# Sixteen expert buffers, a later branch, contiguous rows and unread products around the routing

## The chip, the core and the metric

The kernel runs on one NeuronCore of a Trainium2 chip, as one program. The metric is device time in microseconds of one execution; lower is better. Five engines matter: PE (TensorE), DVE (VectorE), ACT (ScalarE), POOL (GpSimd) and SP (SyncE, which here mostly issues DMA transfers). Each runs its own instructions in order, and they wait for each other through semaphores.

## What is computed

Two transformer blocks on 256 tokens of width 1024, all in fp32. The change lies in the last part of the second block, a mixture of 16 experts:

```python
def hier_moe(h, w_rg, b_rg, w_re, b_re, w1, w3, w2):
    t = h.reshape(-1, d)
    lg = (t @ w_rg + b_rg).astype(jnp.float32)
    g_sel = jnp.argmax(lg, axis=-1)
    w_grp = jnp.take_along_axis(jax.nn.softmax(lg, axis=-1), g_sel[:, None], axis=-1)
    le = (t @ w_re + b_re).astype(jnp.float32).reshape(-1, N_GROUPS, EXPERTS_PER_GROUP)
    le_g = jnp.take_along_axis(le, g_sel[:, None, None], axis=1)[:, 0]
    top_v, top_i = lax.top_k(le_g, TOP_K_IN_GROUP)
    w_top = jax.nn.softmax(top_v, axis=-1) * w_grp
    ...
    def expert_step(acc, xs):
        y = (jax.nn.silu(t @ w1e) * (t @ w3e)) @ w2e
        return acc + ge[:, None] * y, None
...
    x_lat = x_lat + g2 * hier_moe(h2_l, ...)
    return rmsnorm(x_lat, final_g)
```

Each token goes to two of the four experts of one group. One expert has three weight matrices of 2 MiB each (gate, up, down); the 16 experts together have 96 MiB, all of which are read.

## The kernel before

The program runs once through the first block (FFN, attention and recurrence, FFN), then through the second (modulation, attention, output products) and reaches the mixture at about 915 us. There it works in these stages.

**Routing.** The token rows are two tiles x[b] of 128 x 1024. `x_turn` transposes them on PE (trp), `x_high` (L1707) writes a rounded copy of x times its norm into xnh on ACT and `x_low` (L1711) the rest into xnl on DVE; both permute the columns, four interleaved sets per half of 512, so that later reads are contiguous. `logits(b)` (L1716) are eight products of 20 columns (lgp). `pick(b)` (L1726) finds, on DVE, group and ranks and writes m16, two for each token's chosen experts. Three rank products (L1766 to L1768) count the places within the experts, and `one_hot` (L1772) compares them with 0 to 63, so that each expert has 64 places. A token that finds no place is an overflow, counted into novi. The gate weights are worked out beside that by POOL, with one exponential on ACT and one reciprocal on DVE; they end in ghl, which the products gsl (L1810) read.

**Experts.** They go in eight pairs, two experts side by side on PE, each with 64 rows. `gather(p)` (L1788), for two pairs at once, makes the gathered rows, transposed, by one-hot products (gat: for each of eight k four products, weights are columns of xnh and xnl), and evacuates them to xe with scale and shift. Then, per pair: `gate(p)` (pg), `down(p-1)` (yacc), `up(p)` (pu), the gather of the next two pairs if it is due, the transposes of the one-hots (oht), the products that put the rows of p-1 back onto x (scat), and the transposes of the hidden rows (eT, copied by ACT to hT). `down(7)` stands alone at the end. PE's order in this loop is the order of the code.

**Loads.** Each pair has 12 loads of 1 MiB (128 x 2048 fp32), 96 in all, issued by SP from `load_rows` (L234) in the order gate(p), down(p-1), up(p). Buffers are taken in turn from three sets, 5 of tag rawa, 4 of the ring raw that the earlier weights use too, and 4 of rawb: 13. A load whose buffer isn't free makes SP wait, and all behind it.

**Overflow.** `overflow()` (L1895) reads novi into a register on every engine and branches: the body runs the overflowing tokens through all experts, with its own weight loads from SP. With these inputs the count is zero and the body is jumped over. It is called at p == 6, behind hidden_T(6); ahead of it the loads of gate(7), down(6) and up(7) are issued (L2009), and the four of down(7) are issued behind it. On SP the end of the branch also waits for loads in flight.

**End.** `scatter(7)` adds the last rows, then the final RMS norm (squares on ACT, powers on POOL, products on DVE) and four output transfers. The final gain is loaded at about 855 us by POOL into K4[2]. K4 are four fp32 tiles of 128 x 1024.

What sets the order: DVE and ACT stand in the order of the code in the routing (manual schedule `route`), PE in the pair loop; elsewhere a scheduler places instructions by its own estimate.

Of the kernel before, what the change touches and what calls it, by code (L numbers as in the profile page):

```python
# [9 lines left out]
F32 = mybir.dt.float32  # L10
# [23 lines left out]
def constants():  # L34
# [66 lines left out]
    moe={"4": 4, "xe": 2, "oh": 2, "h": 3, "1": 2, "m": 16}, raws=(5, 4, 4))  # L101
# [16 lines left out]
def _body(tc, nc, es, I, out, dbg, stop, R):  # L118
# [116 lines left out]
    def load_rows(src, k):  # L235

        n, i = R["raws"], nraw[0] % sum(R["raws"])
        if i < n[0]:
            raw = P["raw1"].tile([128, 2048], F32, name="rawa", tag="rawa", bufs=n[0])
        elif i < n[0] + n[1]:  # L240
            raw = raw_tile()
        else:
            raw = P["raw2"].tile([128, 2048], F32, name="rawb", tag="rawb", bufs=n[2])
# [189 lines left out]
    x = []  # L433
# [13 lines left out]
    K4 = [cp.tile([128, 1024], F32, name=f"K{i}") for i in range(4)]  # L447
# [1206 lines left out]
    g1b, g2b = K4[1], K4[3]  # L1654
# [22 lines left out]
    route = tc.manual_schedule(engines={mybir.EngineType.DVE, mybir.EngineType.Activation})  # L1677
# [26 lines left out]
    rows4 = lambda t: t.rearrange("p (h q j) -> p h j q", h=2, j=4)  # L1704
    tiles4 = lambda t: t.rearrange("p (h j q) -> p h j q", h=2, j=4)

    def x_high(b):  # L1707
        for h in range(2):
            ACT.activation(tiles4(xnh[b])[:, h], rows4(x[b])[:, h], AF.Copy, scale=rsx[:, b:b + 1])

    def x_low(b):  # L1711
        for h in range(2):
            DVE.scalar_tensor_tensor(tiles4(xnl[b])[:, h], rows4(x[b])[:, h], rsx[:, b:b + 1], tiles4(f32(xnh[b]))[:, h],
                                     op0=OP.mult, op1=OP.subtract)
# [9 lines left out]
    by4 = lambda t: t.rearrange("p b (g e) -> p b g e", g=4)  # L1724

# [19 lines left out]
    for b in range(2):  # L1745
        x_high(b)
        logits(b)
    x_low(0)
# [18 lines left out]
    mm(pr[:, 16:32], ltr[:, 128:256], m16[:, 0, :], start=True, stop=False)  # L1767
    mm(pr[:, 16:32], ltr[:, 0:128], m16[:, 1, :], start=False, stop=True)  # L1768

# [11 lines left out]
    fg = K4[2]  # L1781
    nc.gpsimd.dma_start(fg, bass.AP(tensor=I["final_g_2"].tensor, offset=I["final_g_2"].offset, ap=[[0, 128], [1, D]]))
# [5 lines left out]
    def gather(p):  # L1788

        t = alloc("xe", 2048, "xe", F32, "")  # L1790
        for u in range(2):
            xe[p + u] = lambda k, u=u: t[:, 256 * k + 128 * u:256 * k + 128 * u + 128]
        for k in range(8):
            if k % 2 == 0:
                ps = pa("gat")
            o, s_ = ps[:, 256 * (k % 2):256 * (k % 2) + 256], slice(128 * k, 128 * k + 128)
# [283 lines left out]
```

## Time and profile before

| | us |
|---|---|
| three runs | 1177.48, 1183.94, 1184.63 (median 1183.94) |
| profiled execution | 1180.25 |
| its span on the core | 1178.5 |
| PE busy in the span | 1108.8 (94%) |
| DVE, ACT, POOL busy | 621.2, 477.3, 60.7 |
| bytes moved by DMA | 262.98 MB, mean 223 GB/s |

A profile is one execution, taken by the hardware profiler. A timeline row has the start and the length in us, the engine, the line of the kernel, the operation, the tiles (written <- read), the shape and the count; in brackets how long the engine had stood idle before it and which instruction released it. PE is the product, PEld the load of its weights. A row of a table of stretches has the stretch, its length, the busy time of PE, PEld, DVE, ACT and POOL in it with the instructions in parentheses, PEclk, DMA and GB/s. PEclk is TensorE's granted clock as a share of full speed (1.00 is 2.4 GHz, 0.50 is 1.2 GHz), DMA the busy share of the 16 DMA engines, GB/s what they moved.

### The profile page before, as it was taken

The numbers are of one execution on the slowest core, as the hardware profiler recorded it, in microseconds if no ns is written. First come the engines' busy times: TensorE is split into PE (matmuls) and PEld (weight loads), VectorE is DVE, ScalarE is ACT, GpSimd is POOL, SyncE is SP. The second block draws the span as 40 slices with busy tenths as digits, with TensorE's granted clock in tenths as the row PEclk, the third lists the DMA queues.
The fourth block names the chain that finished last, engine by engine and source line by source line (L and its number), as shares of the span: only waits on it lengthen the run. The fifth ranks groups of instructions, "written<-read, shape, count | busy, mean of one in ns | idle before, by whom it ended". The sixth has DMA issues, their size and how long they took to land. (4 is left out here: it accounts for less than half of the span.)

```text
span 1178.5 us, 17991 instructions
## 1 busy us (share of the span) xinstructions
PE 1108.8 (94%) x7527; PEld 870.1 (74%) x7527; DVE 621.2 (53%) x928; ACT 477.3 (40%) x711; POOL 60.7 (5%) x106
## 2 busy tenths in 40 slices
PE   6999999998988999999999999999899799999976
PEld 6999997887756888999998688888898534343432
DVE  4545545556976556455445865666656603232314
ACT  5444444476643355444444445555544300100002
POOL 1000001000330001000000100000000200000000
PEclk9999999999988999999999999999999799999988
DMA  9855654453557548555556454214285399999984
GB/s 338 275 191 179 198 180 158 157 169 112 179 197 261 197 139 304 195 179 185 175 191 218 153 179 160 72 55 152 96 327 210 145 366 419 421 420 420 421 354 175
DMA packets 119538, 262.98 MB, mean 223 GB/s; under 512 B 6873, under 2 KB 83802, under 8 KB 105242
## 3 DMA queue, kind: packets, MB, share of 16 engines
q1 hardware_dynamic: 118506, 258.88, 60.7%
q0 software_dynamic: 656, 2.36, 0.6%
q8 instruction: 61, 1.00, 0.3%
q10 hardware_dynamic: 288, 0.52, 0.1%
q14 instruction: 27, 0.22, 0.1%
HBM read 260.70 MB, written 1.05 MB: 222 GB/s over the span
## 5 line engine op out<-in xcount | busy, mean ns | idle before, releaser
L263 DVE TENSOR_TENSOR lo<-raw,hi 128x1024 fp32r<-128x1024 f32 x243 | 297.2, 1224 | 285.9 <-ACT hi L262 285.5
L262 ACT ACTIVATE hi<-raw 128x1024 fp32r<-128x1024 f32 x246 | 260.6, 1060 | 318.2 <-PE pj L227 203.3
L227 PE MATMUL pj<-H,hi 128*128 128x256 f32 x752 | 212.4, 283 | 4.1 <-issue 4.1
L226 PE MATMUL pj<-H,hi 128*128 128x256 f32 x752 | 216.2, 288 | 0.0
L228 PE MATMUL pj<-H,lo 128*128 128x256 f32 x752 | 212.4, 282 | 0.4 <-POOL lo L263 0.4
L226 PEld LDWEIGHTS pj<-H,hi 128*128 128x128 f32 x752 | 142.8, 190 | 8.5 <-issue 4.5
L228 PEld LDWEIGHTS pj<-H,lo 128*128 128x128 f32 x752 | 143.0, 190 | 5.2 <-issue 4.5
L227 PEld LDWEIGHTS pj<-H,hi 128*128 128x128 f32 x752 | 142.7, 190 | 1.3 <-issue 0.5
L228 PE MATMUL pj<-hTh,lo 128*128 128x256 f32 x352 | 99.4, 283 | 0.1
L227 PE MATMUL pj<-hTl,hi 128*128 128x256 f32 x352 | 99.2, 283 | 0.0
L226 PE MATMUL pj<-hTh,hi 128*128 128x256 f32 x352 | 99.1, 283 | 0.0
L227 PEld LDWEIGHTS pj<-hTl,hi 128*128 128x128 f32 x352 | 67.3, 192 | 1.3 <-DVE hTl L509 0.8
L226 PEld LDWEIGHTS pj<-hTh,hi 128*128 128x128 f32 x352 | 67.2, 192 | 1.2 <-ACT hTh L508 0.8
L228 PEld LDWEIGHTS pj<-hTh,lo 128*128 128x128 f32 x352 | 67.4, 192 | 0.3 <-DVE lo L263 0.3
L1881 DVE TENSOR_TENSOR yf<-yacc,K 128x512 f32<-128x512 f32 x16 | 11.0, 691 | 104.7 <-PE yacc L1832 82.5
L404 PE MATMUL acc<-lo,hTh 128*128 128x512 f32 x160 | 63.1, 394 | 0.0
L403 PE MATMUL acc<-hi,hTh 128*128 128x512 f32 x160 | 62.7, 392 | 0.0
L407 PE MATMUL acc<-hi,hTl 128*128 128x512 f32 x160 | 49.9, 393 | 0.0
L1832 PE MATMUL pu<-rawa,xe 128*64 128x512 f32 x160 | 45.3, 605 | 0.0
L1864 ACT ACTIVATE hT<-eT 128x512 f32<-128x512 f32 x8 | 4.8, 597 | 91.6 <-PE eT L1863 91.6
L1832 PE MATMUL pg<-raw,xe 128*64 128x512 f32 x128 | 35.8, 595 | 0.0
L1832 PE MATMUL yacc<-rawb,hT 128*64 128x512 f32 x128 | 35.5, 592 | 0.0
(496 smaller groups left out, 1895.2 us busy)
## 6 DMA issues: line engine op xcount, KB each, us to landing
raw<-in_w_in_dram SPq DMA_DIRECT2D x43, 1024.0 KB, 5.1
raw<-in_ffn_up_dram SPq DMA_DIRECT2D x22, 1024.0 KB, 5.2
raw<-in_ffn_down_dram SPq DMA_DIRECT2D x22, 1024.0 KB, 4.9
raw<-in_ffn_gate_dram SPq DMA_DIRECT2D x21, 1024.0 KB, 5.2
rawa<-in_w_exp_up_dram SPq DMA_DIRECT2D x20, 1024.0 KB, 19.2
raw<-in_w_exp_gate_dram SPq DMA_DIRECT2D x16, 1024.0 KB, 14.1
rawb<-in_w_exp_down_dram SPq DMA_DIRECT2D x16, 1024.0 KB, 17.5
raw<-in_w_mod_dram SPq DMA_DIRECT2D x15, 1024.0 KB, 5.0
```

Of the source, the lines that this page charges most:

```text
L226: mm(o, l[0], r[0], start=first, stop=False)
L227: mm(o, l[0], r[1], start=False, stop=False)
L228: mm(o, l[1], r[0], start=False, stop=last)
L262: ACT.activation(hi, r, AF.Copy)
L263: low = lambda: (sub or DVE).tensor_tensor(lo, r, f32(hi), op=OP.subtract)
L403: mm(ps[b][n], hh, wh[:, s_], start=first and f == 0, stop=False)
L404: mm(ps[b][n], hh, wl[:, s_], start=False, stop=False)
L407: mm(ps[b][n], ll, wh[:, s_], start=False, stop=last and f == 1)
L1832: mm(o[halves[u]], l[:, 64 * u:64 * u + 64], r[u], start=first, stop=last, tile_position=(0, 64 * u))
L1864: ACT.activation(t, ps, AF.Copy)
L1881: tt(part(yf, n), yaccs[p][n], part(g2b, n), op=OP.mult)
```

## The change

It has five parts.

- **Buffers.** The expert loads take 16 buffers in turn: 5 rawa, one made of K4[0] and K4[1] (K01), 4 raw, 6 rawb. Room for them comes from smaller pools: tag "4" of the stage from 4 tiles to 2, xe from 2 to 1. g1b moves to a tile of tag "4", yf to K4[2], the tiles of the final norm to xe and K4. The load of the final gain, which sat in K4[2], now goes into K4[0] behind the pair loop.
- **Branch.** overflow() is called at p == 7, behind hidden_T(7) and behind the issue of the down(7) loads, and its body's loads are issued by ACT.
- **Rows.** x_high and x_low no longer permute; each is one instruction of 1024 contiguous elements. The gather reads its weights with a stride of four columns instead.
- **Unread products.** `keep_busy` multiplies ident with g2b into a PSUM tile that nothing reads, 256 or 512 columns wide, at five places between logits and rank products; the routing's written order now covers PE too.
- **Evacuation.** Odd k of the gather are evacuated by ACT, even k by DVE; one_hot(b, 4, 12) stands behind the gather. The first four steps of down(7) come in the order of the other pairs.

```diff
--- before.py
+++ after.py
@@ -98,7 +98,7 @@
     ffn={"4": 16, "2": 11, "1": 2, "m": 12},
     mid={"r4": 9, "r2": 6, "r1": 7, "rm": 16, "v4": 3, "s4": 6, "sm": 6, "gm": 4, "m2": 2, "mm": 2, "pm": 4, "cm": 4, "c1": 2},
     blk={"4": 9, "2": 5, "1": 7, "m": 25}, att={"4": 6, "2": 9},
-    moe={"4": 4, "xe": 2, "oh": 2, "h": 3, "1": 2, "m": 16}, raws=(5, 4, 4))
+    moe={"4": 2, "xe": 1, "oh": 2, "h": 3, "1": 2, "m": 16}, raws=(5, 1, 4, 6))
 
 
 class Stop(Exception):
@@ -238,9 +238,11 @@
         if i < n[0]:
             raw = P["raw1"].tile([128, 2048], F32, name="rawa", tag="rawa", bufs=n[0])
         elif i < n[0] + n[1]:
+            raw = K01
+        elif i < n[0] + n[1] + n[2]:
             raw = raw_tile()
         else:
-            raw = P["raw2"].tile([128, 2048], F32, name="rawb", tag="rawb", bufs=n[2])
+            raw = P["raw2"].tile([128, 2048], F32, name="rawb", tag="rawb", bufs=n[3])
         nraw[0] += 1
         nc.sync.dma_start(raw, src.rearrange("(p k) n -> p (k n)", k=k))
         return raw
@@ -444,7 +446,8 @@
                        channel_multiplier=-1)
 
     H = [cp.tile([128, 1024], F32R, name=f"H{i}") for i in range(4)]
-    K4 = [cp.tile([128, 1024], F32, name=f"K{i}") for i in range(4)]
+    K01 = cp.tile([128, 2048], F32, name="K01")
+    K4 = [K01[:, 0:1024], K01[:, 1024:2048]] + [cp.tile([128, 1024], F32, name=f"K{i}") for i in (2, 3)]
     nhalf = cp.tile([128, 32], F32, name="nhalf")
     POOL.memset(nhalf, -0.5)
     nones = cp.tile([128, 128], F32, name="nones")
@@ -1651,7 +1654,7 @@
     att.close()
     P["raw1"] = es.enter_context(tc.tile_pool(name="raw1", bufs=1, side="right", reuse_waits="tile"))
 
-    g1b, g2b = K4[1], K4[3]
+    g1b, g2b = t4("gb"), K4[3]
     part = lambda t, n: t[:, 512 * n:512 * n + 512]
     for n in range(2):
         ACT.activation(part(g1b, n), mod_bcast(mhl[0], n), AF.Copy)
@@ -1674,7 +1677,7 @@
     L, rsx = cp.tile([128, 2, 20], F32, name="L"), cp.tile([128, 2], F32, name="rsx")
     xnh, xnl, xT = H[0:2], H[2:4], [t4("xT") for _ in range(2)]
     pl = pa("lgp")
-    route = tc.manual_schedule(engines={mybir.EngineType.DVE, mybir.EngineType.Activation})
+    route = tc.manual_schedule(engines={mybir.EngineType.DVE, mybir.EngineType.Activation, mybir.EngineType.PE})
     route.__enter__()
 
     def x_add(b):
@@ -1701,17 +1704,12 @@
                 ACT.activation(part(xT[b], kh), ps, AF.Copy)
 
 
-    rows4 = lambda t: t.rearrange("p (h q j) -> p h j q", h=2, j=4)
-    tiles4 = lambda t: t.rearrange("p (h j q) -> p h j q", h=2, j=4)
 
     def x_high(b):
-        for h in range(2):
-            ACT.activation(tiles4(xnh[b])[:, h], rows4(x[b])[:, h], AF.Copy, scale=rsx[:, b:b + 1])
+        ACT.activation(xnh[b], x[b], AF.Copy, scale=rsx[:, b:b + 1])
 
     def x_low(b):
-        for h in range(2):
-            DVE.scalar_tensor_tensor(tiles4(xnl[b])[:, h], rows4(x[b])[:, h], rsx[:, b:b + 1], tiles4(f32(xnh[b]))[:, h],
-                                     op0=OP.mult, op1=OP.subtract)
+        DVE.scalar_tensor_tensor(xnl[b], x[b], rsx[:, b:b + 1], f32(xnh[b]), op0=OP.mult, op1=OP.subtract)
 
     def logits(b):
         for k in range(8):
@@ -1722,6 +1720,11 @@
     rk, sel = cp.tile([128, 2, 5, 4], F32, name="rk"), cp.tile([128, 2, 4], F32, name="sel")
     m16 = cp.tile([128, 2, 16], F32R, name="m16")
     by4 = lambda t: t.rearrange("p b (g e) -> p b g e", g=4)
+
+    def keep_busy(n, w=512):
+
+        for _ in range(n):
+            mm(pa("busy")[:, 0:w], ident, g2b[:, 0:w], start=True, stop=True)
 
     def pick(b):
         DVE.scalar_tensor_tensor(L[:, b], pl[:, 32 * b:32 * b + 20], rsx[:, b:b + 1], rbias, op0=OP.mult, op1=OP.add)
@@ -1745,6 +1748,8 @@
     for b in range(2):
         x_high(b)
         logits(b)
+        keep_busy(1, 256)
+    keep_busy(2)
     x_low(0)
     pick(0)
     x_low(1)
@@ -1765,7 +1770,9 @@
     pr = pa("rank")
     mm(pr[:, 0:16], ltr[:, 0:128], m16[:, 0, :], start=True, stop=True)
     mm(pr[:, 16:32], ltr[:, 128:256], m16[:, 0, :], start=True, stop=False)
+    keep_busy(2)
     mm(pr[:, 16:32], ltr[:, 0:128], m16[:, 1, :], start=False, stop=True)
+    keep_busy(1, 256)
 
     oh = [alloc("oh", 1024, "oh", F32R, "") for _ in range(2)]
 
@@ -1778,8 +1785,6 @@
         one_hot(b, 0, 4)
     pr16 = big("pr16")
     DVE.tensor_copy(pr16, pr[:, 0:32].rearrange("p (b n) -> p b n", b=2))
-    fg = K4[2]
-    nc.gpsimd.dma_start(fg, bass.AP(tensor=I["final_g_2"].tensor, offset=I["final_g_2"].offset, ap=[[0, 128], [1, D]]))
     gsl = sm("gsl", 8)
     novi = mp.tile([1, 1], I32, name="novi", tag="novi", bufs=1)
     xe, hps, yaccs, hTs, backs = {}, {}, {}, {}, {}
@@ -1790,16 +1795,21 @@
         t = alloc("xe", 2048, "xe", F32, "")
         for u in range(2):
             xe[p + u] = lambda k, u=u: t[:, 256 * k + 128 * u:256 * k + 128 * u + 128]
+        pss = pc2("gat") + pc2("gat") if p == 0 else [None] * 4
         for k in range(8):
-            if k % 2 == 0:
-                ps = pa("gat")
-            o, s_ = ps[:, 256 * (k % 2):256 * (k % 2) + 256], slice(128 * k, 128 * k + 128)
+            ps = pss[k // 2] = pss[k // 2] or pa("gat")
+            o, g = ps[:, 256 * (k % 2):256 * (k % 2) + 256], t[:, 256 * k:256 * k + 256]
             for i, w in enumerate((xnh, xnl)):
                 for b in range(2):
-                    mm(o, w[b][:, s_], oh[b][:, 128 * p:128 * p + 256], start=i + b == 0, stop=i + b == 2)
-            DVE.tensor_scalar(t[:, 256 * k:256 * k + 256], o, sc2p[:, k:k + 1], sh2p[:, k:k + 1], op0=OP.mult, op1=OP.add)
-            if p == 0 and k in (1, 3):
-                one_hot(k // 2, 4, 12)
+                    mm(o, w[b][:, 512 * (k // 4) + k % 4:512 * (k // 4) + 512:4], oh[b][:, 128 * p:128 * p + 256],
+                       start=i + b == 0, stop=i + b == 2)
+            if k % 2:
+                ACT.activation(g, o, AF.Identity, bias=sh2p[:, k:k + 1], scale=sc2p[:, k:k + 1])
+            else:
+                DVE.tensor_scalar(g, o, sc2p[:, k:k + 1], sh2p[:, k:k + 1], op0=OP.mult, op1=OP.add)
+        if p == 0:
+            for b in range(2):
+                one_hot(b, 4, 12)
 
     def places():
 
@@ -1869,14 +1879,14 @@
         raws = ahead.pop((p, 2), None) or fetch(p, 2)
         steps = [(f, n) for f in range(4) for n in range(2)]
         if p == 7:
-            steps.sort(key=lambda v: v[1])
+            steps[4:] = [(2, 0), (3, 0), (2, 1), (3, 1)]
         for f, n in steps:
             o = 1024 * (f % 2) + 512 * n
             pair_mm(yaccs[p][n], hTs[p][:, 128 * f:128 * f + 128], [r[:, o:o + 512] for r in raws[f // 2]], f == 0, f == 3)
 
     def scatter(p):
 
-        yf, yh_, yl_ = t4("yf"), t4("yh", F32R), t4("yl", F32R)
+        yf, yh_, yl_ = K4[2], t4("yh", F32R), t4("yl", F32R)
         for n in range(2):
             tt(part(yf, n), yaccs[p][n], part(g2b, n), op=OP.mult)
             ACT.activation(part(yh_, n), part(yf, n), AF.Copy)
@@ -1897,7 +1907,7 @@
         def some(w, k, i, n):
 
             t = t4("few")
-            nc.sync.dma_start(t.rearrange("p (k n) -> p k n", k=n), w.rearrange("(p k) n -> p k n", k=k)[:, i:i + n])
+            nc.scalar.dma_start(t.rearrange("p (k n) -> p k n", k=n), w.rearrange("(p k) n -> p k n", k=k)[:, i:i + n])
             return t
 
         nov = nc.values_load(novi, min_val=0, max_val=512)
@@ -1905,16 +1915,16 @@
             e_ = mybir.EngineType
             with tc.manual_schedule(engines={e_.PE, e_.DVE, e_.Activation, e_.Pool, e_.SP}):
...
@@ -2005,14 +2014,16 @@
             if add:
                 add()
             hTs[p] = hidden_T(hps[p], alloc("h", 512, "hT", F32, ""))
-            if p == 6:
-                ahead.update({k: fetch(*k) for k in ((7, 0), (6, 2), (7, 1))})
+            if p == 7:
+                ahead[7, 2] = fetch(7, 2)
                 overflow()
         down(7)
         scatter(7)()
 
 
-    xn, sq = [t4("xn") for _ in range(2)], t4("sq")
+    fg, sq, xn = K4[0], K4[1], alloc("xe", 2048, "xn", F32, "")
+    nc.gpsimd.dma_start(fg, bass.AP(tensor=I["final_g_2"].tensor, offset=I["final_g_2"].offset, ap=[[0, 128], [1, D]]))
+    xn = [xn[:, 0:1024], xn[:, 1024:2048]]
     rs, ss = [sm("rs", 1) for _ in range(2)], [sm("ss", 2) for _ in range(2)]
     for n in range(2):
         for b in range(2):
```

The places at which the order of instructions moves, as the engines' programs have them. First PE from the transposes of the rows to the first gathered rows (trp, lgp, rank and gat as above; busy are the unread products). Before:

```order
L1697 MATMUL trp<-ident,x_72 128x128 x8
L1718 MATMUL lgp<-wr,xT 128x20 x16
L1766 MATMUL rank<-m_8820,ltr 128x16
L1767 MATMUL rank<-m_8820,ltr 128x16
L1768 MATMUL rank<-m_8820,ltr 128x16
```

And of the change, same place:

```order
L1700 MATMUL trp<-ident,x_72 128x128 x8
L1716 MATMUL lgp<-wr,xT 128x20 x8
L1727 MATMUL busy<-K_84,ident 128x256
L1716 MATMUL lgp<-wr,xT 128x20 x8
L1727 MATMUL busy<-K_84,ident 128x256
L1727 MATMUL busy<-K_84,ident 128x512 x2
L1771 MATMUL rank<-m_8820,ltr 128x16
L1772 MATMUL rank<-m_8820,ltr 128x16
L1727 MATMUL busy<-K_84,ident 128x512 x2
L1774 MATMUL rank<-m_8820,ltr 128x16
L1727 MATMUL busy<-K_84,ident 128x256
```

Seven unread products stand between the logits, the rank products and the gather.

Second PE in the change from the last pair's gate products to the last down products (the body of the branch is left out). The branch stands between the last transposes (eT) and yacc of pair 7; before, the same two rows of it stood behind the eT of pair 6, ahead of the gate products of pair 7.

```order
L1842 MATMUL pu<-raw,xe 64x512 x8
L1842 MATMUL pu<-rawb,xe 64x512 x8
L1836 MATMUL oht<-ident,oh 128x128 x2
...
L1873 MATMUL eT<-ident,hp 128x128 x4
L1913 TENSOR_LOAD novi
L1914 COMPARE_AND_BRANCH
...
L1914 UNCONDITIONAL_BRANCH x2
L1842 MATMUL yacc<-rawb,hT 64x512 x16
```

Third SP, the queue of the loads. Before, the end of its program is (the body left out):

```order
L245 DMA rawb<-in_w_exp_up_dram 128x2048 x3
L245 DMA rawa<-in_w_exp_up_dram 128x2048
L1903 TENSOR_LOAD novi
L1904 COMPARE_AND_BRANCH
...
L1904 UNCONDITIONAL_BRANCH x2
L1903 ISA x2
L245 DMA rawa<-in_w_exp_down_dram 128x2048 x4
L2035 DMA out_dram<-xn 128x512 x2
```

And of the change:

```order
L247 DMA rawb<-in_w_exp_up_dram 128x2048 x2
L247 DMA rawb<-in_w_exp_down_dram 128x2048 x4
L1913 TENSOR_LOAD novi
L1914 COMPARE_AND_BRANCH
L1914 UNCONDITIONAL_BRANCH x2
L1913 ISA x2
L2046 DMA out_dram<-xn 128x512 x2
```

The last four loads moved from behind the branch to ahead of it, and the body's loads are gone from SP's program.

## Rows read from the trace of the kernel before

**Rows 1.** Table of stretches: busy us by engine, then PEclk, DMA share, GB/s.
```profile
915.00:920.00 5.00, 4.71 (x40) 4.39 (x39) 3.81 (x6) 4.12 (x8) 2.05 (x4) 0.97 0.71 252
920.00:925.00 5.00, 2.88 (x13) 2.70 (x13) 3.99 (x11) 2.57 (x3) 0.00 (x0) 0.50 1.01 416
935.00:940.00 5.00, 4.36 (x13) 1.63 (x14) 1.86 (x3) 0.00 (x0) 0.00 (x0) 0.68 0.00 0
970.00:1120.00 150.00, 142.29 (x692) 60.73 (x690) 45.57 (x78) 13.46 (x22) 0.00 (x0) 1.00 1.01 420
1127.00:1129.00 2.00, 0.00 (x0) 0.00 (x0) 0.00 (x0) 0.00 (x0) 0.00 (x0) 0.72 1.06 410
1133.00:1135.00 2.00, 2.00 (x8) 0.67 (x6) 0.00 (x0) 0.00 (x0) 0.00 (x0) 0.57 1.04 422
1146.00:1148.00 2.00, 2.00 (x12) 0.78 (x10) 0.56 (x1) 0.00 (x0) 0.00 (x0) 1.00 0.02 8
```

**Rows 2.** Timeline of SP's queue, expert loads around the two gaps.
```profile
917.00 0.56 SPq L245 DMA_DIRECT2D rawb<-in_w_exp_down_dram  x1
942.37 1.99 SPq L245 DMA_DIRECT2D rawa<-in_w_exp_down_dram  x2
...
1147.75 2.04 SPq L245 DMA_DIRECT2D rawa<-in_w_exp_down_dram  x4
```

**Rows 3.** PE's largest wait, 942 to 1125 us: us in total, times, longest.
```profile
PE gat L1799 <- DVE xe L1800: 7.7, 12, 0.7
```

**Rows 4.** The branch's line: durations in ns (least, median, most), starts in us.
```profile
L1904 PEldq COMPARE_BRANCH  x1: 6164/6164/6164, 1124.1 to 1124.1; - x1
```

**Rows 5.** Timeline of PE around the branch and at the end.
```profile
1130.71 4.77 PE L1832 MATMUL pg<-rawa,xe 128*64 128x512 f32 x12 [6.30 <-PEq L1904]
...
1155.57 0.63 PE L1863 MATMUL eT<-ident,hp 128*128 128x128 f32 x4
1156.88 2.79 PE L1832 MATMUL yacc<-rawa,hT 128*64 128x512 f32 x10 [0.69 <-ACT hT L1864]
1160.13 5.36 PE L1832 MATMUL yacc<-rawa,hT 128*64 128x512 f32 x22 [0.46 <-DMA rawa<-in_w_exp_down_dram]
```

**Rows 6.** Timeline of DVE, routing.
```profile
922.35 0.24 DVE L1727 SCALAR_TENSOR_TENSOR L<-lgp,rsx,rbias 128x20 f32<-128x20 f32 x1 [0.80 <-PE lgp L1718]
...
924.16 2.14 DVE L1713 SCALAR_TENSOR_TENSOR H<-x,rsx,H 128x512 fp32r<-128x512 f32 x2
```

**Rows 7.** Timeline of PE, routing.
```profile
917.47 4.84 PE L1718 MATMUL lgp<-wr,xT 128*128 128x20 f32 x32
...
928.17 0.38 PE L1768 MATMUL rank<-m,ltr 128*128 128x16 f32 x1 [3.21 <-DVE m L1738]
929.16 3.76 PE L1799 MATMUL gat<-oh,H 128*128 128x256 f32 x16 [0.60 <-DVE oh L1773]
```

**Rows 8.** Timeline of PE, the gather of pairs 2 and 3.
```profile
980.97 0.73 PE L1799 MATMUL gat<-oh,H 128*128 128x256 f32 x4
982.37 1.21 PE L1799 MATMUL gat<-oh,H 128*128 128x256 f32 x8 [0.67 <-DVE xe L1800]
...
987.92 0.74 PE L1799 MATMUL gat<-oh,H 128*128 128x256 f32 x4 [0.64 <-DVE xe L1800]
```

**Rows 9.** The page's costliest groups: count, busy us and mean ns of one.
```profile
L263 DVE TENSOR_TENSOR lo<-raw,hi 128x1024 fp32r<-128x1024 f32 x243 | 297.2, 1224 | 285.9 <-ACT hi L262 285.5
```

**Rows 10.** Timeline of ACT, then of POOL: exponential, and first step behind the reciprocal.
```profile
931.50 0.21 ACT L1972 ACTIVATE ed<-ed 128x10 f32<-128x10 f32 x1 [8.93 <-POOL ed L1947]
...
943.73 0.20 POOL L1978 TENSOR_TENSOR ed<-ed,den 128x2 f32<-128x2 f32 x1 [10.66 <-DVE den L1977]
```

**Rows 11.** Weight loads by shape: 970 to 1120 us, last row 915 to 925.
```profile
L1799 PEld LDWEIGHTS gat<-oh,H 128*128 128x128 f32 x96 | 12.3, 188 | 12.6 <-DVE xe L1800 10.2 <-issue 2.4
...
L1863 PEld LDWEIGHTS eT<-ident,hp 128*128 128x128 f32 x20 | 3.1, 201 | 0.4
...
L1697 PEld LDWEIGHTS trp<-ident,x 128*128 128x128 f32 x16 | 1.8, 140 | 0.6 <-PE trp L1697 0.5
```

More of the change, by code (lines that the diff above doesn't have):

```diff
@@ L1907, in overflow @@
                 for b in range(2):
-                    t, xT = t4("yf"), t4("yh")
+                    t, xo = K4[2], alloc("xe", 2048, "xo", F32, "")
+                    xT, hp, hT = xo[:, 0:1024], xo[:, 1024:1536], xo[:, 1536:2048]
                     tt(t, f32(xnh[b]), f32(xnl[b]), op=OP.add)
@@ L1911, in overflow @@
                         ps = pa("gat")
-                        PE.transpose(ps[:, 0:128], t[:, 128 * k:128 * k + 128], ident)
+                        PE.transpose(ps[:, 0:128], t[:, 512 * (k // 4) + k % 4:512 * (k // 4) + 512:4], ident)
                         DVE.tensor_scalar(xT[:, 128 * k:128 * k + 128], ps[:, 0:128], sc2p[:, k:k + 1], sh2p[:, k:k + 1],
@@ L1916, in overflow @@
                     for e in range(16):
-                        hp = part(t4("hp"), 0)
                         for i in range(2):
@@ L1927, in overflow @@
                                 ACT.activation(hp, ps, AF.Silu)
-                        hT = hidden_T(hp, part(t4("hT"), 0))
+                        hidden_T(hp, hT)
                         for f in range(4):
@@ L1932, in overflow @@
                                 mm(acc[n], hT[:, 128 * f:128 * f + 128], part(raw, n), start=e + f == 0, stop=e == 15 and f == 3)
-                    t = t4("yf")
                     for n in range(2):
```

## The prediction

> **What bounds the kernel now.** The change touches only the last quarter, the mixture of experts, so I read that stretch alone, in four steps.
>
> First the table by stretches [rows 1]. It shows three phases. From 915 to 945 us the routing runs: the granted clock is 0.50 between 920 and 925 and 0.68 between 935 and 940, and in that last stretch the DMA engines carry nothing (0 GB/s). From 970 to 1120 they carry 420 GB/s with TensorE at full clock and 142.29 of 150 us busy, so one load of 1 MiB takes 1.049 MB / 420 GB/s = 2.50 us. Behind 1146 DMA falls to 8 GB/s for 2 us, though loads are still missing.
>
> Second, the queue that issues the loads [rows 2]. The thirteenth leaves at 917.0 and the fourteenth only at 942.37, when TensorE has finished with the first buffer. The last four leave only at 1147.75: they stand behind the branch on SP, and DMA has run dry by then.
>
> Third, whether those DMA gaps cost anything. The waits of TensorE from 942 to 1125 [rows 3] are led by the evacuation of the gather, 7.7 us in 12 waits; no expert load is among them. So from the first release at 942.37 the end is a chain of TensorE's own work. What stands outside it are two rows: the branch, 6.30 us in which TensorE waits [rows 4, 5], and at the end 0.69 us for hT and 0.46 us for the last load [rows 5]. The DMA gap around 1146 costs 0.46 us, not 4.
>
> Fourth, what sets 942.37. The logits are 32 products in 4.84 us up to 922.31; VectorE waits 0.80 us for them, takes up pick(0) at 922.35 and x_low(1) at 924.16 (2.14 us), and then pick(1) [rows 6]; the last rank product is at 928.17, the gather starts at 929.16 [rows 7]. Gather and first gate products then take 929.16 to 942.37, 13.2 us, at clocks of 0.50 to 0.68; the same gather in a calm stretch runs from 980.97 to 988.5, 7.5 us with four waits of 0.64 to 0.67 [rows 8].
>
> **The change, part by part.** All against the profiled execution: span 1178.5 plus 1.75 outside it, 1180.25 us. The three other runs go from 1177.48 to 1184.63, median 1183.94.
>
> 1. *Logits to gather.* x_high and x_low become one contiguous instruction of 1024 elements each. VectorE's contiguous subtraction of that size takes 1.22 us [rows 9], x_low now 2.14 to 2.23: 0.9 us less on the path from pick(0) to pick(1). (x_high is off the path: ACT's next work there is at 931.5 [rows 10].) The unread products are 3 of 256 columns and 4 of 512, 5.5 times 512. A 512 column record costs 5.36/22 = 0.24 us [rows 5]; a full fp32 product is between one and four such records (0.24 to 0.97), and I take 0.9, since two half-wide fp32 products are already recorded as four. That makes 5 us in all at full clock, 10 at half.
> If the clock holds: the products before the fall (the clock fell within 915 to 920, where the mean is 0.97, so near 919.7) ran at full level for 2.2 us and the rest, 2.6 us, at half; at full level 1.3. Logits end at 917.47 + 2.2 + 1.3 + 0.45 (one unread product between them) = 921.4. pick(0) takes 1.85 (922.35 to 924.16, with its last instruction's tail), x_low 1.25, pick(1) 1.9: 926.4. Beside that TensorE does 256 + 2 x 512 unread columns, 2.25 us, until 923.7, where rank(0) is due at 923.3; then 2 x 512, 1.8 us, until 925.6: hidden. Rank and one-hots take 1.0 as before (928.17 to 929.16); the last unread 256 columns lie beside the one-hots. The gather starts at 927.4, 1.8 earlier.
>
> 2. *Gather to first release.* The routing order now covers TensorE: five gate products stand in three of the gather's waits (5 x 0.43 = 2.15 against 1.9 us, so 0.2 over), two more are needed after it (0.9): 7.5 + 0.2 + 0.9 + 0.1 = 8.7 us at full clock. Release at 936.1 instead of 942.37, **6.3 us earlier**. Odd tiles are evacuated by ACT: a change of engine, not of the waits. The exponential behind those evacuations moves from 931.50 to about 936; then five POOL steps (1.1), the reciprocal and six more steps (1.4, from 943.73 on [rows 10]) give the gates at about 939, a microsecond before TensorE has done its remaining nine gate products (3.9 us). No new wait, but little room.
>
> 3. *Sixteen buffers.* Three more loads, 7.5 us, run in the hole of 927 to 942. All 16 have landed at about 935; 80 x 2.50 = 200 us more, with a slow start as now, puts the last landing at release + 205. That is no gain by itself, as TensorE didn't wait for loads. It keeps DMA from becoming the bound once TensorE is earlier. The final gain's 0.5 MB load moves behind the last use of its buffer, 1.2 us of DMA beside the tail.
>
> 4. *Branch.* Before, from release to the end of eT(7): 942.37 to 1156.2, 213.8 us. It holds the branch (6.3) and what half clock cost behind it: the clock falls at 1127.9 (0.72 over 1127 to 1129) and rises at 1134.7 (0.57 over 1133 to 1135) [rows 1], TensorE works again from 1130.71, so 4.0 us at half, 2.0 lost. Without both: 205.5. All of it returns behind eT(7): branch 6.3 in place of the 0.69 wait, down(7) 32 records, about 7.5, plus 2.0 for half clock. All 96 loads are now issued ahead of the branch, so the 0.46 falls. From the last down product (1165.5) to the end stays 13.0.
>
> Sum: 936.1 + 205.5 + 6.3 + 9.5 + 13.0 = 1170.4, plus 1.75 = **1172 us**, 8 less than the profiled execution: 6.3 of it from the routing, 1.8 from the tail.
>
> One price is open on both sides. The gather's weight columns become strided by four. The nearest rows are loads of weights at stride two, 201 ns (eT), and contiguous, 140 (trp) and 188 (the gather itself) [rows 11]: between 0 and 61 ns more each, over 128 loads 0 to 7.8 us. I take 0, since the gather's own contiguous loads are near the strided ones already. The Trainium skill, "TensorE: Matmul & The Clock Gate", section "Step-by-step: what each phase is for", has the time of a weight load scale with the column count alone, which would leave the sum as it is; the 61 ns between eT and trp speak against it.
>
> **The rivals.**
>
> *Clock not held.* Nothing in the trace shows that these few unread products hold the clock; it fell while TensorE was issuing logits without a pause. Then the logits end at 922.3 plus 0.4; 2.25 us of products last 4.5, until 927.2, and hold up rank(0); the next two take 1.8 to 3.6, until 929 to 930.8, and rank(1), due at 927.3, waits for them. Gather at 930 to 932. With the clock back by then, release at 938.7 to 940.7, end at 1174.6 to 1176.6. With the low gather of now (13.2) nothing is gained: up to 1181.
>
> *A shorter branch.* The fetch ran while DMA carried 410 GB/s [rows 1]; now TensorE gets there at about release + 206, when the loads have just landed. The floor is 0.7 (hT has to be copied), if the target were there at once. At 2 us the clock might not fall either: it fell at 1127.9, 3.5 us behind the last product. 4.3 + 2.0 less: 1166. Against it: the compare-and-branch itself took 6164 ns on TensorE [rows 4]. The Trainium skill, "Runtime: NRT & Kernel Launch", section "Instruction fetch mechanics", says that a taken branch whose target is not in the current window of two pages must fetch the target page by DMA first; by it the stall stays wherever the branch is put, which is the sum's 1172, and it may appear on ACT too, whose branch body now issues the loads; ACT's next work is then only at the end of down(7).
>
> *Loads bind after all.* The last up(7) load lands at release + 193 to 196, and TensorE wants it from about release + 196. A slow start of DMA could cost 0 to 4 us: 1172 to 1176. This lies within the forecast's range.
>
> *Slower: strided weights.* If stride four adds twice what stride two does (122 ns), and none of it hides, 128 loads cost 15.6 us: 1188. It decides from 8.1/128 = 63 ns on. For it: 201 against 140. Against: the gather's products stand 0.15 us apart (8 in 1.21) though their loads take 188 [rows 8, 11], so loads overlap; and four waits per gather hide some.
>
> **How the numbers follow.** Forecast 0.47 (its own range 1168 to 1177), clock not held 0.25, shorter branch 0.15, strided weights or another loss 0.13 (half of it above 1182). The range 1163 to 1182 leaves out the far ends of the last two. One per cent, 12 us, is about what can be told from no change here. From the profiled 1180 the forecast is 0.7% faster, from the median 1.0%: so it is shared. Faster by over 1%: 0.35 (the shorter branch, and a part of the forecast); within 1%: 0.56; slower: 0.09.
>
> **What would show it.** After: the granted clock from 915 to 936 (1.00, or 0.5 in a stretch); the seventeenth load at about 936 rather than 942; the gather's start (927.4) and length (8 to 9 us); TensorE's branch row, 6 us or less, and where; no wait for a load in pair 7; mean weight load of the gather, 188 ns or over 200; last down product to end 13 us. I am wrong if the release is later than 940, if the branch costs under 3 us, or if a wait for loads or for the gates of over 2 us shows up.

## The result and the profile after

The changed kernel took 1193.83 us (median of 4 runs, 1192.15 to 1197.26) against 1182.03 for the kernel before: ratio 1.0108, interval 1.0074 to 1.0141. It is 1.1% slower, where 0.7 to 1.0% faster was forecast, and outside the range that was given. The profiled execution took 1197.26 us, its span 1195.5.

One thing has to be set aside first. The stage starts with the first transposes of the rows (trp), at 915.25 us in the profile before and at 919.34 after, though TensorE's work ahead of it is the same. Over all thirteen profiles of this study that point lies between 912.29 and 921.00, whatever the kernel (last section). So below I count from the first trp: before 263.25 us to the end of the span, after 276.16, 12.9 more.

The stage's TensorE rows after, as in [rows 5], [rows 7] and [rows 8] (timeline: start, us, engine, line, what, count, idle time before it with what ended it; PEq is TensorE's sequencer, which takes the branch):

```profile
919.34 1.47 PE L1700 MATMUL trp<-ident,x 128*128 128x128 f32 x12
...
926.65 4.58 PE L1727 MATMUL busy<-K,ident 128*128 128x256 f32 x6
...
932.60 0.57 PE L1774 MATMUL rank<-m,ltr 128*128 128x16 f32 x1
...
933.81 1.27 PE L1804 MATMUL gat<-oh,H 128*128 128x256 f32 x4
...
985.94 1.21 PE L1804 MATMUL gat<-oh,H 128*128 128x256 f32 x4
987.79 2.24 PE L1804 MATMUL gat<-oh,H 128*128 128x256 f32 x8 [0.64 <-DVE xe L1809]
...
996.47 1.31 PE L1804 MATMUL gat<-oh,H 128*128 128x256 f32 x4 [0.64 <-DVE xe L1809]
997.58 0.63 PE L1836 MATMUL oht<-ident,oh 128*128 128x128 f32 x2
...
1168.78 0.63 PE L1873 MATMUL eT<-ident,hp 128*128 128x128 f32 x4
1173.41 8.76 PE L1842 MATMUL yacc<-rawb,hT 128*64 128x512 f32 x32 [4.00 <-PEq L1914]
```

Eight products of the gather take 2.24 us where they took 1.21 [rows 8], with the same waits of 0.64 between them. The gather of pairs 2 and 3 goes from 985.94 to 997.58, 11.6 us instead of 7.5. The weight loads show where it comes from (by shape, 970 to 1120 us: count, busy us, mean ns), against 188 ns in [rows 11]:

```profile
L1804 PEld LDWEIGHTS gat<-oh,H 128*128 128x128 f32 x96 | 23.7, 328 | 13.2 <-DVE xe L1809 10.8 <-issue 2.4
```

And behind it the clock (table of stretches; the third value from the end is the granted clock):

```profile
949.00:985.00 36.00, 35.00 (x166) 12.92 (x164) 4.58 (x12) 3.08 (x6) 1.26 (x7) 0.95 0.96 389
985.00:1002.00 17.00, 14.45 (x51) 11.67 (x48) 5.76 (x10) 2.26 (x4) 0.00 (x0) 0.62 0.98 409
```

In the kernel before it was 1.00 from 970 to 1120 [rows 1]. In each of the three later gathers it now falls to half, and the products that follow (oht, scat, eT) run at half level until it comes back. The three gathers are 4.11, 4.06 and 4.02 us longer, the stretches from oht to the next pg 2.2, 1.1 and 2.0: 17.5 us in all.

The rest, by the sum's own terms, from the first trp on. The fourth column is the experiment a_rows_back, told next:

| term | forecast | after | permuted rows | before |
|---|---|---|---|---|
| first trp to gather | 12.2 | 14.47 | 14.48 | 13.91 |
| gather to first release | 8.7 | 14.29 | 9.82 | 13.21 |
| release to end of eT(7) | 205.5 | 221.3 | 202.1 | 213.8, branch in it |
| wait ahead of down(7) | 6.3 | 4.00 | 3.46 | 0.69 |
| down(7) | 9.5 | 8.76 | 8.79 | 8.61 |
| to the end of the span | 13.0 | 13.3 | 13.4 | 13.0 |
| sum | 255.2 | 276.1 | 252.0 | 263.3 |

### The profile page after: what moved, and what is told of

It reads as the page before. It is cut to its first block, busy times and chain, and to the rows that moved or that the text cites. A ratio compares the mean times of both kernels' runs of the same rounds, so it can differ in the third digit from the quotient of the medians.

```text
span 1195.5 us, 18031 instructions
## 1 busy us (share of the span) xinstructions
PE 1137.1 (95%) x7541; PEld 893.6 (75%) x7541; DVE 613.3 (51%) x910; ACT 484.2 (40%) x725; POOL 60.8 (5%) x106
## 5 line engine op out<-in xcount | busy, mean ns | idle before, releaser
L1891 DVE TENSOR_TENSOR K<-yacc,K 128x512 f32<-128x512 f32 x16 | 11.1, 691 | 100.8 <-PE yacc L1842 100.8
L1804 PEld LDWEIGHTS gat<-oh,H 128*128 128x128 f32 x128 | 31.7, 328 | 17.7 <-DVE xe L1809 13.2
L1804 PE MATMUL gat<-oh,H 128*128 128x256 f32 x128 | 36.6, 441 | 8.4 <-DVE xe L1809 8.3
L1807 ACT ACTIVATE xe<-gat,sh2p,sc2p 128x256 f32<-128x256 f32 x16 | 9.0, 564 | 67.4 <-PE gat L1804 67.4
L409 PEld LDWEIGHTS acc<-hi,hTl 128*128 128x128 f32 x160 | 30.1, 188 | 6.9
## 6 DMA issues: line engine op xcount, KB each, us to landing
rawb<-in_w_exp_up_dram SPq DMA_DIRECT2D x12, 1024.0 KB, 12.9
```

Of the source, the lines that this page charges most:

```text
L409: mm(ps[b][n], ll, wh[:, s_], start=False, stop=last and f == 1)
L1804: mm(o, w[b][:, 512 * (k // 4) + k % 4:512 * (k // 4) + 512:4], oh[b][:, 128 * p:128 * p + 256], start=i + b == 0, stop=i + b == 2)
L1807: ACT.activation(g, o, AF.Identity, bias=sh2p[:, k:k + 1], scale=sc2p[:, k:k + 1])
L1891: tt(part(yf, n), yaccs[p][n], part(g2b, n), op=OP.mult)
```

## The experiments

Medians, ratios to the kernel before with their intervals, and from the first trp to the end in the profile:

| kernel | median | ratio | interval | from trp |
|---|---|---|---|---|
| changed | 1193.83 | 1.0108 | 1.0074 to 1.0141 | 276.2 |
| a_rows_back | 1173.32 | 0.9911 | 0.9880 to 0.9943 | 252.0 |
| b_rows_only | 1194.28 | 1.0088 | 1.0067 to 1.0109 | 276.1 |
| a_no_busy | 1192.11 | 1.0064 | 1.0041 to 1.0088 | 272.2 |
| a_rows_back_no_busy | 1173.27 | 0.9918 | 0.9897 to 0.9938 | 254.2 |
| a_stride2 | 1172.16 (1 run) | | | 251.4 |
| a_busy_gather | 1186.15 | 1.0040 | 1.0019 to 1.0061 | 268.5 |
| b_branch_late | 1183.79 | 1.0014 | 0.9992 to 1.0037 | 265.2 |
| a_extra_loads | 1183.17 (1 run) | | | 266.6 |
| a_branch_last | 1170.38 | 0.9903 | 0.9864 to 0.9941 | 249.7 |
| a_best | 1168.57 | 0.9886 | 0.9862 to 0.9911 | 250.4 |
| a_best_no_busy | 1172.26 | 0.9902 | 0.9876 to 0.9928 | 251.2 |

**The rows, taken back and alone.** The theory was that the stride of four in the gather's weights costs all of it; the rival, that buffers, branch or unread products do.

```diff
 a_rows_back, against the changed kernel
-        ACT.activation(xnh[b], x[b], AF.Copy, scale=rsx[:, b:b + 1])
+        for h in range(2):
+            ACT.activation(tiles4(xnh[b])[:, h], rows4(x[b])[:, h], AF.Copy, scale=rsx[:, b:b + 1])
...
-                    mm(o, w[b][:, 512 * (k // 4) + k % 4:512 * (k // 4) + 512:4], oh[b][:, 128 * p:128 * p + 256],
+                    mm(o, w[b][:, 128 * k:128 * k + 128], oh[b][:, 128 * p:128 * p + 256],
```

> The changed kernel with permuted rows again: x_high and x_low write four interleaved column sets as in the kernel before, and the gather's weight columns are contiguous. Theory S, the stride costs: the gathers of pairs 2, 4 and 6 took 11.6 us instead of 7.5 and the clock stayed low behind them; they lose 4.1 each and 1 to 2 us behind each, 17.5 us in all, so this kernel is at 1193.8 - 17.5, plus about 1 for the slower x_low: 1175 to 1178, ratio to before 0.993 to 0.997; weight loads of the gather at 190 to 210 ns, clock 1.00 from 960 to 1120. Rival, the loss comes from the buffers, the branch or the unread products (other parts of the change that let the clock fall): 1190 to 1194, ratio 1.008 to 1.012, the clock still falls at the gathers.

It took 1173.32 us, 20.5 less than the changed kernel, 0.9% below the kernel before and 1.7 below the range of theory S. The weight load is back at 188 ns, eight products at 1.22 us, and the clock holds (by shape; timeline; table of stretches):

```profile
L1810 PEld LDWEIGHTS gat<-oh,H 128*128 128x128 f32 x96 | 12.4, 188 | 12.6 <-DVE xe L1815 10.2 <-issue 2.4
```

```profile
978.62 1.22 PE L1810 MATMUL gat<-oh,H 128*128 128x256 f32 x8 [0.66 <-DVE xe L1815]
```

```profile
960.00:1120.00 160.00, 152.28 (x744) 65.51 (x742) 43.09 (x72) 21.14 (x36) 0.00 (x0) 1.00 1.01 421
```

That is 24.1 us from the first trp on: 17.5 in and behind the later gathers, 4.5 in the first one, 1.7 more up to eT(0), where the changed kernel runs at half clock, and 0.5 in the branch. The converse, the kernel before with the rows alone (the same two edits the other way):

> The kernel before with nothing but the contiguous x_high and x_low and the stride of four in the gather's weights. Theory S: 17.5 us more in and behind the later gathers, 1 to 3 more in the first, 1 less before it: 1198 to 1203, ratio 1.014 to 1.018. Rival (stride hidden, loss elsewhere): 1181 to 1183, ratio 0.999 to 1.001.

1194.28 us, 9.9 above the kernel before (1184.35 in the runs beside it), fewer than the 16 to 21 expected. The weight loads are at 329 ns (by shape, 970 to 1130 us):

```profile
L1793 PEld LDWEIGHTS gat<-oh,H 128*128 128x128 f32 x96 | 23.8, 329 | 13.1 <-DVE xe L1794 10.7 <-issue 2.4
```

Its later gathers cost 5.3, 5.8 and 5.1 us up to the eT behind them, 16.2 in all. The other terms went the other way: the first gather cost nothing up to the first eT (0.5 less than before), up(5) took 7.0 us where it had taken 8.0, and down(7) is 1.5 shorter, with no wait for a load in it. From trp on 12.8 are left. The direction is shown; what the stride is worth in the kernel before I had overestimated.

**Which part is the stride, which the clock.** First the stride's distance:

```diff
 a_stride2, against the changed kernel
-                    mm(o, w[b][:, 512 * (k // 4) + k % 4:512 * (k // 4) + 512:4], oh[b][:, 128 * p:128 * p + 256],
+                    mm(o, w[b][:, 256 * (k // 2) + k % 2:256 * (k // 2) + 256:2], oh[b][:, 128 * p:128 * p + 256],
```

> The changed kernel with weight columns of the gather at stride two instead of four; this gathers other columns than the ones wanted, so its values are not the reference's, the work is the same in kind and amount. Price by stride: if it grows with the distance, a weight load of 235 (a third of the way from 188 to 329), gather 8.5 to 9 us, total 1178 to 1184. If any stride pays the whole: 329, 11.6 us, 1192. If two is nearly free, as the rows of eT suggested (201): 190 to 210, 7.5 to 8 us, 1173 to 1176.

At stride two a weight load takes 196 ns, the later gathers 7.6 us, the kernel 1172.16 (weight loads by shape, 925 to 1180 us; timeline):

```profile
L1804 PEld LDWEIGHTS gat<-oh,H 128*128 128x128 f32 x128 | 16.9, 196 | 16.3 <-DVE xe L1809 13.3 <-issue 2.9
```

```profile
980.09 1.23 PE L1804 MATMUL gat<-oh,H 128*128 128x256 f32 x8 [0.65 <-DVE xe L1809]
```

This kernel differs from the changed one in nothing but the stride, so the loss is the stride's. Two is nearly free and four is not; the price does not grow with the distance in a line. Then the clock, held by one unread product in each wait of the strided gathers:

```diff
 a_busy_gather, against the changed kernel
                 DVE.tensor_scalar(g, o, sc2p[:, k:k + 1], sh2p[:, k:k + 1], op0=OP.mult, op1=OP.add)
+                if p:
+                    keep_busy(1, 256)
```

> The changed kernel, stride four as it is, with one more unread product of 256 columns in each of the four waits of the gathers of pairs 2, 4 and 6. It splits the 17.5 us that these gathers lost: 12.2 in the gathers, 5.3 behind them at half clock. If the weight loads set the gather's pace by themselves and the clock is a second, separate loss: gathers stay at 11.3 to 12, the products behind them go at full clock, 1188 to 1190. If the half clock is what made the gather long: gathers of 8 to 9 us, 1179 to 1183. If the clock falls all the same: 1193 to 1196.

1186.15 us, 7.7 less than the changed kernel and 2 below the range of the case that it bears out, the first. The gather of pairs 2 and 3 is at 11.3 us, its weight loads at 328, but the products behind it run at full clock:

```profile
981.86 0.59 PE L1727 MATMUL busy<-K,ident 128*128 128x256 f32 x2
982.66 2.17 PE L1804 MATMUL gat<-oh,H 128*128 128x256 f32 x8 [0.21 <-DVE xe L1809]
...
992.56 0.40 PE L1902 MATMUL scat<-yl,back 128*128 128x512 f32 x1
```

Eight products take 2.17 us at full clock and 2.24 to 2.26 where the clock was at half. The weight loads set the gather's pace at either level, and the clock is a second loss, which an unread product in each wait takes away. Of the 17.5 us, some 11.3 are the stride's own and 6 the clock's.

**The unread products.** The edit: `keep_busy` loops zero times.

> The changed kernel without the seven unread products. Theory S says nothing of them beyond the routing: they delayed the last rank product by 0.8 us and the logits by 0.5 to 1; the gather's first part may run at half clock without them, where its weight loads set the pace: 1192 to 1197. Rival, the unread products are a good part of the loss (their 8 us of PE at half clock delay the rank): 1185 to 1190.

> Permuted rows and no unread products in the changed kernel. With theory S for the stride, this against the same with unread products (1175 to 1178) is what they bring where the gather is at full speed. If they hold the clock: this one 3 to 6 us slower, 1179 to 1183. If they only delay the rank: 1 to 2 us faster, 1174 to 1176.

With the stride they cost in these two profiles: 1192.11 us without, and 4.0 less from trp on. The gather's start is delayed by 1.9 us (14.47 against 12.61), and the gather, bound by its weight loads, gains nothing from the clock. With permuted rows the medians are the same (1173.3, just below the range for a mere delay), and the profiles say 2.2 us in their favour (252.0 against 254.2): the gather starts 0.5 later and then runs at full clock. They don't hold the clock in the logits there: in a_rows_back it is 0.72 and 0.60 from 920 to 930 and 1.00 from 930 on.

```profile
920.00:925.00 5.00, 5.00 (x29) 4.70 (x29) 3.37 (x7) 4.15 (x4) 0.67 (x2) 0.72 0.87 301
925.00:930.00 5.00, 5.00 (x9) 2.15 (x8) 4.29 (x14) 0.00 (x0) 0.53 (x3) 0.60 0.98 392
930.00:935.00 5.00, 4.27 (x20) 2.34 (x18) 1.94 (x5) 0.56 (x1) 2.98 (x16) 1.00 1.01 426
```

But that goes by the execution. In a_stride2, which has the changed kernel's routing, the clock held (table of stretches; timeline), and the gather starts 12.19 us behind its first trp (918.97), not 14.47:

```profile
920.00:925.00 5.00, 4.71 (x42) 4.45 (x40) 3.17 (x4) 4.09 (x8) 0.86 (x2) 1.00 0.77 239
925.00:930.00 5.00, 4.54 (x15) 2.06 (x14) 4.31 (x16) 0.00 (x0) 0.00 (x0) 1.00 1.00 408
```

```profile
931.16 0.93 PE L1804 MATMUL gat<-oh,H 128*128 128x256 f32 x4
```

It held through logits and rank products in a_extra_loads too, whose routing is that of a_rows_back, and fell in the five other profiles with unread products. So a pair of profiles says little on what they are worth. Up to eT(0), the four with permuted rows and unread products take 39.0 to 40.9 us from trp, the two without 41.3 and 41.4.

**The branch.** TensorE waited 3.35 to 4.0 us for it behind the last products in the six kernels so far that have it there, and its row was 6.16 in its old place [rows 4]. Is it the place?

```diff
 b_branch_late, against the kernel before
-            if p == 6:
-                ahead.update({k: fetch(*k) for k in ((7, 0), (6, 2), (7, 1))})
+            if p == 7:
+                ahead[7, 2] = fetch(7, 2)
                 overflow()
```

> The kernel before with one part of the change alone: the branch behind the last gate and up products and behind the issue of all loads (13 buffers, permuted rows, body's loads still on SP). If the fetch is shorter because the loads have drained by then (3.4 to 4.0 us in the late place, 6.16 in the early one): 2.5 to 3 less, and 0.5 to 1.2 from the load and hT waits at the end: 3 to 4 us, ratio 0.9965 to 0.9975. If the late place is not what shortened it: 6.2 us again, 0 to 1 us less, ratio 0.999 to 1.000.

No gain (1.0014). With 13 buffers the loads are later, and two things change: TensorE waits 3.7 us in the last pairs, 2.4 of it put down to loads and 1.3 to SP's line of the branch, where SP waits for loads in flight (waits of TensorE, 942 to 1182 us), and they are still running as the branch starts at 1153.9, which then takes 5.69 us (branch's line, ns; table of stretches):

```profile
PE pu L1832 <- DMA rawb<-in_w_exp_up_dram: 1.4, 1, 1.4
PE pu L1832 <- SPq L1904: 1.3, 1, 1.3
PE yacc L1832 <- DMA rawb<-in_w_exp_down_dram: 1.0, 1, 1.0
```

```profile
L1904 PEldq COMPARE_BRANCH  x1: 5688/5688/5688, 1153.9 to 1153.9; - x1
```

```profile
1154.00:1156.00 2.00, 0.27 (x3) 0.07 (x1) 1.09 (x2) 0.60 (x1) 0.00 (x0) 1.00 0.99 373
```

To tell place from traffic, eight more loads ahead of the branch, with sixteen buffers:

```diff
 a_extra_loads, against a_rows_back
                 ahead[7, 2] = fetch(7, 2)
+                for i in range(2):
+                    fetch(0, i)
                 overflow()
```

> The changed kernel with permuted rows and eight more loads of 1 MiB, read by nothing, queued behind the last expert load and ahead of the branch, so that DMA is still full when TensorE takes the branch. If the fetch is long because it stands among loads: compare-and-branch of 5.5 to 6.3 us instead of 3.48, as at the early place (6.16) and at the late place with 13 buffers (5.69). If the place in the program decides it: 3.3 to 4.0. The total is longer in either case, since the engines' end of the branch waits for loads in flight.

Same place, same code but for the loads, DMA full: 6.00 us. Without the extra loads, in a_rows_back: 3.48, with DMA at 127 GB/s and falling. The branch's line and the table of stretches, first with the extra loads:

```profile
L1920 PEldq COMPARE_BRANCH  x1: 6002/6002/6002, 1142.8 to 1142.8; - x1
```

```profile
1144.00:1146.00 2.00, 0.00 (x0) 0.00 (x0) 0.00 (x0) 0.00 (x0) 0.00 (x0) 1.00 1.02 422
```

And without:

```profile
L1920 PEldq COMPARE_BRANCH  x1: 3476/3476/3476, 1142.9 to 1142.9; - x1
```

```profile
1144.00:1146.00 2.00, 0.00 (x0) 0.00 (x0) 0.01 (x1) 0.00 (x0) 0.00 (x0) 1.00 0.32 127
```

So traffic decides, not the place. The profile also shows a packet that the branch waits for. It has queues that it calls instruction, and one packet of q8, 0.02 MB, starts within each of these two branch rows (DMA queues in 0.1 us: packets, MB, share of 16 engines' time). In a_rows_back, from 1143.8 to 1143.9:

```profile
q8 instruction: 1, 0.02, 68.2%
```

And in a_extra_loads, from 1146.3 to 1146.4:

```profile
q8 instruction: 1, 0.02, 67.1%
```

A packet stands at its start with its whole time, here 1.1 us (68.2% of 16 times 0.1 us). It starts 1.0 us into the branch without the extra loads and 3.5 us into it with them, and in both the branch ends 1.4 us behind its end (the packets of the other such queue, q14, show no fixed distance). In twelve of the thirteen profiles the branch ends 1.4 to 1.5 us behind the end of the last such packet; in the changed kernel the packet takes 1.6 us, hence 3.99. In b_branch_late, where two such packets run side by side, the distance is 2.0. That agrees with what the Trainium skill says in "Runtime: NRT & Kernel Launch", "Instruction fetch mechanics", of a target page fetched by DMA; that it takes 2.5 us longer among loads is from these rows. The buffers and the branch belong together: sixteen buffers let the loads run out by the time it is taken.

**A faster kernel.** With permuted rows, the branch behind the last scatter:

```diff
 a_branch_last, against a_rows_back
-                overflow()
         down(7)
         scatter(7)()
+        overflow()
```

> The changed kernel with permuted rows (1173.3) and the branch moved once more: behind the last scatter, ahead of the final norm, so that TensorE has nothing left to do behind it. Theory: only TensorE pays for the branch (3.46 us of waiting, and about 2 for the half clock behind it), the other engines 0.05 to 0.07 us; then 3.46 - 0.69 (the wait for hT comes back) + 2.0 = 4.8 less, 0.5 to 1 more for reading the register on the engines of the tail: 1169 to 1170, ratio 0.988. Rival, the other engines' cheap branches were cheap because they had idle time to fetch in: 3 to 6 us on the tail, 1172 to 1176.

1170.38 us; from trp on 2.3 less than a_rows_back, not 4 to 5. TensorE's part came as expected (0.69 in place of 3.46, down(7) 7.09 instead of 8.79), but the squares and products of the final norm, which lay beside the last scatter, now stand behind the branch, and down(7)'s end to the end of the span takes 15.6 us instead of 13.4. DVE's products (timeline) are put down to TensorE's branch, which ends at 1153.4, so in this profile the tail waits for it too:

```profile
1151.04 0.69 DVE L1907 TENSOR_TENSOR x<-x,scat 128x512 f32<-128x512 f32 x1 [0.17 <-PE scat L1906]
1153.56 1.90 DVE L2038 TENSOR_TENSOR xn<-x,K 128x512 f32<-128x512 f32 x3 [1.82 <-PEq L1920]
```

Then, besides, a PSUM tile for each k in the later gathers, so that odd products don't wait for the evacuation of the even ones, with and without the unread products:

```diff
 a_best, against a_branch_last
-            ps = pss[k // 2] = pss[k // 2] or pa("gat")
-            o, g = ps[:, 256 * (k % 2):256 * (k % 2) + 256], t[:, 256 * k:256 * k + 256]
+            if p:
+                o = pa("gat")[:, 0:256]
+            else:
+                o = pss[k // 2][:, 256 * (k % 2):256 * (k % 2) + 256]
+            g = t[:, 256 * k:256 * k + 256]
```

> The changed kernel with permuted rows, the branch behind the last scatter, and one PSUM tile for each k in the gathers of pairs 2, 4 and 6, so that odd products don't wait for the evacuation of the even ones (7.7 us in 12 waits with permuted rows). If TensorE's chain alone sets the end: 7.5 less than with the branch last (1170.4), 1162 to 1164, ratio 0.981 to 0.984. If the loads bind now (their last landing was at 1145 in the profile with permuted rows, 2 us behind TensorE's last transposes, and they can't come sooner): TensorE waits 3 to 5 us for loads in the last two pairs, 1165 to 1168, ratio 0.985 to 0.988.

> The same without the seven unread products. In the profiles with permuted rows they made the stretch from the first transposes to the end 2.2 us shorter (252.0 against 254.2), while the medians did not differ (1173.3 both). If the 2.2 are real: 1.5 to 3 us slower than its sibling. If the loads bind, the earlier release moves them too, and the same holds. If they bring nothing: within 1 us.

1168.57 us, 1.1% below the kernel before and the lowest median here, 0.6 above the range for the case in which loads bind. The later gathers went from 7.5 to 3.9 us, 10.9 in all, and most of it did not arrive: TensorE now waits 5.4 us in the last pairs (waits of TensorE from 925 us on), 3.3 of it put down to loads and 2.1 to SP's line of the branch, where SP waits for loads in flight.

```profile
PE pu L1851 <- SPq L1923: 2.1, 1, 2.1
PE yacc L1851 <- DMA raw<-in_w_exp_down_dram: 1.3, 1, 1.3
PE pu L1851 <- DMA rawb<-in_w_exp_up_dram: 1.3, 1, 1.3
PE yacc L1851 <- DMA K<-in_w_exp_down_dram: 0.7, 1, 0.7
```

By its median it is 1.8 us below a_branch_last, whose runs were not taken beside it; in the profiles it is 0.7 longer from trp on, with its gather's start the same and its eT(0) 1.7 later. So what the extra tiles bring is open. The unread products are worth 3.7 us by the two medians, whose runs were taken together, and 0.8 by the profiles; the intervals of the two ratios overlap, and with the tiles as they were the medians did not differ. A gain is likely, and not shown.

## Why the prediction was wrong

**The step that failed is the price of the strided weight columns**, "I take 0, since the gather's own contiguous loads are near the strided ones already". It was bounded by rows at stride two (201 ns), and stride two is indeed nearly free (196); four is not (328). The rival had the mechanism with 122 ns on 128 loads; measured are 140 ns. Two things in its working were off. The argument against it, "so loads overlap", held for loads of 188 ns with products 0.15 us apart; with loads of 328 the products stand 0.28 us apart, so 130 of the 140 ns arrive. And the rival had no clock: the slower gather lets the clock fall, 6 of the 17.5 us. It got 0.13, half of it above 1182; the range should have reached to its price, 1188.

**Logits to release** was mis-sized too. The clock did not hold in the profile of the changed kernel, nor in that with permuted rows: there the rival "clock not held" is what happened. Put on the forecast's scale, with the first trp at 915.25, the last rank product starts at 928.5 and the gather at 929.7 in both, just short of the rival's 930, and 0.6 later than before. With permuted rows the release comes at 939.6, inside the rival's 938.7 to 940.7 and not at 936.1; in the changed kernel the strided gather puts it at 944.0. Where the clock did hold, in a_stride2, the first term is 12.19, the forecast's 12.2; so which of the two cases comes goes by the execution, and nothing here says what decides it. But the release is 9.9 us behind the gather's start there too, 9.8 with permuted rows, not 8.7: the gather with five gate products in its waits took about 1 us more than a calm one, where 0.2 was taken. x_low came out as worked out (1.28 us).

**From release on** the sum held where the stride did not reach: 202.1 with permuted rows (forecast 205.5, in which I had left the half clock behind the first gather and 1.1 us of up(5)), down(7) 8.8 with its half clock, 13.4 behind it. The shorter branch, given 0.15, came half way: 3.5 to 4.0 us where the sum took 6.3 and the rival 2, for the reason that it named, drained loads; the half clock stayed, and ACT's branch took 0.05 us, so nothing of the stall moved there. Loads did not bind, and no wait for the gates showed up. With permuted rows, misses of 3.8 us later (routing, gather, tail) and 7.0 earlier (from release on, branch, down(7)) partly cancel: 252.0 against 255.2, and 1173.3 us against 1172. That agreement is partly luck.

## What to carry to other kernels

An operand that is read many times should be laid out once for its reader: the permutation that the change saved cost 0.9 us, and the strided reading that it brought 20 by the medians and 24 by the profiles. Price a stride at its own distance; the row at half of it said nothing. Where an engine waits at a branch that jumps over its body, put the branch where transfers have drained, and give it the buffers that let them; a gain on one engine then shows which resource binds next.

## What the runs showed of the hardware

- A weight load of 128 columns in this gather takes 188 ns contiguous, 196 at stride two, 328 at stride four. The Trainium skill, "TensorE: Matmul & The Clock Gate", "Step-by-step: what each phase is for", ties its time to the count of columns alone; here the stride decides. The strided pace is the same at either level of the clock (2.17 and 2.26 us for eight products).
- TensorE's compare-and-branch took 3.35 to 4.0 us where DMA had drained or was draining (nine profiles) and 5.7 to 6.2 where it was full as the branch began (four). In twelve of the thirteen it ended 1.4 to 1.5 us behind a packet of the queue q8 instruction. The other engines' took 0.045 to 0.072 in all of them.
- The clock fell in a stretch in which TensorE is recorded busy for 14.45 of 17 us, most of it the strided gather; with one unread product in each wait it did not. From the logits to the rank products the unread products held it in two profiles of seven.
- The first trp lies between 912.29 and 921.00 us over thirteen profiles. It goes in part with the granted clock between 300 and 400 us, far ahead of the change: 0.95 at 912.29, 0.93 at 915.25 and 914.95, 0.91 at 919.21 and 919.34, 0.90 at 921.00 (others, as 0.91 at 915.00 and 0.95 at 916.77, don't fit). So a difference of 2 or 3 us between kernels is better read from the profile, counted from the first trp, than from few medians; and even there the clock in the logits moves the gather's start by 2 us between executions of the same routing (12.19 and 14.47).
